# A two-layer Fourier and RG-LRU trunk on one core: position rows loaded by DMA, the first stage in another order, two weight sums on VectorE, zero-frequency columns written at once

## The chip, the cores and the metric

The kernel runs on one core of one Trainium2 chip. The metric is the device time of one execution in microseconds (us). Engines are named as in the profile: PE (TensorE matmuls), PEld (its weight loads), DVE (VectorE), ACT (ScalarE), POOL (GpSimd), and SPq, the queue on which SyncE issues all DMAs.

## What is computed

128 prompt tokens and 1024 sample tokens of width 1024 pass two layers. Only layer 0 and its input matter here. The position embedding is added to the sample tokens alone: its first 512 columns depend on the row of a token in a 64-wide grid, its last 512 on the column.

```python
xs = x_sample + _grid_pos_embed(...)           # rows: sin, cos(r*omega); columns: sin, cos(c*omega)
h  = _rmsnorm(x, norm_g) * (1 + scale) + shift # shift, scale, gate = split(silu(cond) @ w_ada + b_ada)
u, z = split(h @ w_in)
f  = real(fft2(u, axes=(tokens, 256 channels of a group), norm="ortho"))
y  = einsum("bsgi,gij->bsgj", f, w_fmix) + b_fmix
x  = x + gate * ((y * silu(z)) @ w_out)
```

## The kernel before

Every wide product is three matmuls on a value split in a high part (`...h`, rounded by ACT) and the rest (`...l`, by DVE): helper `mm3`, lines 238 to 240, or the same by hand.

The **first stage** transforms the tokens before they meet `w_in`. Token tiles `x0` (prompt) to `x8` get their position rows and their norm; `x1..x4` are paired with `x5..x8` into a difference `d0..d3` and a sum that stays in place. `psO` are the products of the differences with DFT tables (`dh`, `dl` from `dr`), one PSUM tile for each of 8 column blocks; `psT` and `psF` do the same on differences and sums of the sums. ACT and DVE scale them by `coef` and write them as `Qo` and `Qr`, the transformed tokens. Beside this `fold` multiplies the DFT of the channels into `w_fmix` (tiles `wf`, results `Ah Al Bh Bl R`), and `ada_part` computes scale (`s0..s3`) and shift (`h0..h3`) from 16 tiles `wada`: eight matmuls for a pair of tiles, then a copy `hot` (ACT), a small product `adc` (PE) and `coef` (DVE).

The first stage is planned: class `Plan` puts DVE, ACT and POOL operations in order by costs written in the code; where an operation has two costs, it may go to DVE or POOL. PE and the DMA queue keep the order of three strings. `DORD` is the order of loads (`x` token tiles, `w` the `wf`, `t` DFT tables, `s` and `h` the `wada`, `p` position rows, `L` the first pair of `w_u0`). `PORD` and `RORD` are the order on PE: `j` pairs of tiles, `f` folds, `t62` means 6 column blocks with `d2`, `u52` block 5 with `d0, d1`, `o` the eviction into `Qo`, `q` the `psT`, `F` the `psF`, `U` the first two products `pu` of the mixer. Buffers are few: two `dr`, three `raw` (for `wf`, the second half of `wada`, `w_u0`), four `xs` (`x5..x8` and the first half of `wada`), eight PSUM banks. A load waits on SPq for its buffer, and everything behind it waits too.

Position rows come as one 80x512 table. DVE marks six one-hot blocks in `hot`, six matmuls spread the table over 128 tokens, ACT copies four of the results to SBUF, two stay in PSUM. `pos0` and `pos1` add them to a tile; `pos0` is tied to DVE.

The **mixer** runs over 8 channel groups g: `umat(g)` (`pu`) multiplies `Qo` and `Qr` by the sums and differences `e`, `o` of two weight tiles `uL`, `uR` (made by `uweights(g+1)` on POOL), `ymat(g-1)` applies `A`, `B`, `R` and stores `y`. In g=0, `prologue` computes the Nyquist channel (`nyq`, `Ucat`) and a row of norm factors `rb` from nine diagonal blocks `dg`. `norm_stream`, three (chunk, k) pairs per g, makes the normed tokens for z on POOL (`nt`) and stores them in `hD`; after g=7 they are loaded again (`hr`, `hh`, `hl`) for the z stage. Here and after, the Tile framework's scheduler orders each engine. `zero(c)` overwrites the zero-frequency columns of `Qr[c]` from `k0r`, high part and rest, in two small DVE operations for each of 8 column blocks.

Of the kernel before, what the change touches and what calls it, by code (L numbers as in the profile page):

```python
# [187 lines left out]
def body(tc, nc, a):  # L188
# [211 lines left out]


    hot = xp.tile([128, 512], F32, name="hot")
    posR, posC = [None] * 4, [None] * 2
    for n, (kind, i) in enumerate((("R", 0), ("C", 0), ("R", 2), ("C", 1), ("R", 1), ("R", 3))):
        oh = hot[:, i * 128:i * 128 + 128]
        lo, hi = (0, 64) if kind == "C" else (64, 80)

        def mark(kind=kind, i=i, oh=oh, lo=lo, hi=hi):
            if kind == "C":
                e = ident[lo:hi, 32 * i:32 * i + 32].rearrange("p (o c) -> p o c", o=1).broadcast_to([64, 4, 32])  # L410
            else:
                e = ident[lo:hi, 64 + 4 * i:68 + 4 * i].rearrange("p (r o) -> p r o", o=1).broadcast_to([16, 4, 32])
            V.tensor_copy(oh[lo:hi].rearrange("p (r c) -> p r c", r=4), e)

        def spread(n=n, kind=kind, i=i, oh=oh, lo=lo, hi=hi):
            T["ps", f"p{n}"] = ps(f"pos{kind}{i}")
            PE.matmul(T["ps", f"p{n}"], oh[lo:hi], T["dr", "pos"][lo:hi], start=True, stop=True)
# [2 lines left out]
        if kind == "R" and i % 2 == 0:  # L420
            posR[i] = ("ps", f"p{n}")
        else:
            key = (posC if kind == "C" else posR)[i] = ("pos" + kind, i)

# [1149 lines left out]
```

## Time and profile before

| | |
|---|---|
| three runs | 1504.72 us median (1499.46 to 1507.64) |
| the profiled execution | 1498.54 us, of which the span is 1496.8 us |
| PE, DVE, ACT, POOL busy in it | 97%, 72%, 49%, 11% |

The span runs from the first to the last instruction. Shares are means over stages with different limits: a change in one stage is read from the waits in that stage. The granted clock column shows 1.00 also where no record exists, as in the first 20 us.

### The profile page before, as it was taken

What the parts mean: (1) busy time and instruction counts of PE and PEld (TensorE: products, weight loads), DVE (VectorE), ACT (ScalarE), POOL (GpSimd) and SP (SyncE); (2) the same over time, 40 slices, a digit from 0 to 9 for tenths busy, and PEclk for the clock granted to TensorE, in tenths of its full rate; (3) what the DMA queues carried; (4) which work ended last, traced back from release to release, by engine and by line L of the source; (5) the groups of instructions that cost most, each with busy time, mean ns of one, the idle gap of its engine ahead of it and who ended that gap; (6) DMA issues with size and microseconds to landing.
All of it is one profiled execution on the core that took longest, in us unless ns stands there. A gap on an engine that the chain in (4) does not pass through costs nothing. (4 is left out here: it accounts for less than half of the span.)

```text
span 1496.8 us, 21486 instructions
## 1 busy us (share of the span) xinstructions
PE 1452.2 (97%) x8370; PEld 1414.3 (94%) x8370; DVE 1073.2 (72%) x1596; ACT 740.5 (49%) x1113; POOL 157.5 (11%) x165
## 2 busy tenths in 40 slices
PE   7888999999999999999999999999999999999996
PEld 4578999999999999999999999999999999899996
DVE  7775455798864486747888787878788888686453
ACT  6552233322222354526866666666675758464331
POOL 2026785000001001000000000000000000000000
PEclk9998999999999999999999999999999999999998
DMA  6643657887665567531111111111111111786451
GB/s 222 200 130 117 178 188 266 302 269 247 223 212 162 184 195 240 187 126 43 59 59 60 57 59 58 59 59 58 59 59 59 59 58 65 231 287 206 148 189 48
DMA packets 83926, 212.73 MB, mean 142 GB/s; under 512 B 11424, under 2 KB 42656, under 8 KB 83696
## 3 DMA queue, kind: packets, MB, share of 16 engines
q1 hardware_dynamic: 83824, 211.36, 43.2%
q8 instruction: 65, 1.06, 0.3%
q14 instruction: 37, 0.30, 0.1%
HBM read 171.98 MB, written 39.35 MB: 141 GB/s over the span
## 5 line engine op out<-in xcount | busy, mean ns | idle before, releaser
L270 DVE SCALAR_TENSOR_TENSOR sil1j<-wada,sil 128x1024 bf16<-128x1024 f32 x64 | 78.1, 1220 | 9.9 <-DMA wada<-w_ada 9.8
L1289 DVE SCALAR_TENSOR_TENSOR uc<-u,tab,uc 128x1156 f32<-128x1156 f32 (+2 forms) x54 | 69.3, 1288 | 15.7 <-ACT u L1272 14.4
L1348 DVE SCALAR_TENSOR_TENSOR nu<-ga,nu 128x1156 f32<-128x1156 f32 x32 | 43.5, 1358 | 47.4 <-ACT tr L1343 47.3
L1107 DVE SCALAR_TENSOR_TENSOR x<-o,ada,xr 128x128 f32<-128x128 f32 (+1 forms) x64 | 31.6, 513 | 58.1 <-PE o L240 57.5
L1326 ACT ACTIVATE tr<-g,gb 128x386 f32<-128x386 f32 (+1 forms) x96 | 54.8, 584 | 22.0 <-PE g L240 21.0
L227 ACT CAST gh<-gr 128x384 fp32r<-128x384 f32 x80 | 39.7, 511 | 49.6 <-DMA gr<-gD 48.4
L1275 ACT ACTIVATE uc<-u,tab 128x386 f32<-128x386 f32 (+1 forms) x48 | 32.3, 673 | 61.4 <-PE u L240 61.4
L792 POOL TENSOR_TENSOR xr<-xr,tab 128x384 f32<-128x384 f32 (+1 forms) x24 | 23.0, 961 | 367.6 <-DMA xr<-xT 334.3
L228 DVE TENSOR_TENSOR gl<-gr,gh 128x384 fp32r<-128x384 f32 x80 | 42.1, 555 | 24.0 <-ACT gh L227 24.0
L1401 ACT ACTIVATE szz<-zz 128x386 f32<-128x386 f32 (+1 forms) x48 | 23.6, 495 | 71.9 <-PE zz L240 71.8
L1371 POOL COPY st<-nu 128x1 f32<-128x1 f32 x16 | 6.8, 426 | 495.5 <-DVE nu L1370 495.4
L888 ACT CAST uh<-pu 128x256 fp32r<-128x256 f32 (+1 forms) x32 | 12.7, 398 | 84.9 <-PE pu L240 84.8
L1326 ACT ACTIVATE ti<-g,gb 128x386 f32<-128x386 f32 (+1 forms) x96 | 51.6, 579 | 5.8 <-PE g L240 5.7
L889 DVE TENSOR_TENSOR ul<-pu,uh 128x256 fp32r<-128x256 f32 (+1 forms) x32 | 14.4, 454 | 49.7 <-ACT uh L888 49.6
L1358 DVE SCALAR_TENSOR_TENSOR ti<-ti,uc 128x1156 f32<-128x1156 f32 x32 | 43.5, 1358 | 7.6 <-ACT ti L1326 7.3
L1332 ACT ACTIVATE nu<-tr,sp2p 128x1156 f32<-128x1156 f32 x32 | 43.5, 1358 | 1.5 <-ACT tr L1326 0.4
L1354 DVE SCALAR_TENSOR_TENSOR tr<-ga,tr 128x1156 f32<-128x1156 f32 x32 | 43.5, 1361 | 0.7
L1362 DVE TENSOR_TENSOR ti<-ti,tr 128x1156 f32<-128x1156 f32 x32 | 43.4, 1357 | 0.4
L1336 ACT ACTIVATE ga<-tr,sm 128x1156 f32<-128x1156 f32 x32 | 43.2, 1349 | 0.1
L1373 DVE TENSOR_TENSOR_SCAN nu<-ga,tab,ti 128x1155 f32<-128x1155 f32 x16 | 41.9, 2619 | 0.1
L1370 DVE TENSOR_TENSOR_SCAN nu<-ga,ti 128x1156 f32<-128x1156 f32 x16 | 40.9, 2559 | 0.3
L227 ACT CAST gh<-sz 128x384 fp32r<-128x384 f32 x16 | 8.2, 514 | 63.1 <-DVE sz L1009 63.1
(1818 smaller groups left out, 5611.1 us busy)
## 6 DMA issues: line engine op xcount, KB each, us to landing
wo<-w_out SPq DMA_DIRECT2D x96, 512.0 KB, 4.2
wz<-w_z SPq DMA_DIRECT2D x32, 512.0 KB, 4.3
wada<-w_ada SPq DMA_DIRECT2D x32, 512.0 KB, 4.3
gr<-gD SPq DMA_DIRECT2D x80, 192.0 KB, 4.2
yD<-y SPq DMA_DIRECT2D x16, 576.0 KB, 4.8
zy<-yD SPq DMA_DIRECT2D x16, 576.0 KB, 6.9
wada<-w_adaN SPq DMA_DIRECT2D x16, 512.0 KB, 5.4
wu<-w_u SPq DMA_DIRECT2D x16, 512.0 KB, 3.6
```

The source lines that it names most:

```text
L227: A.copy(hi, src)
L228: (eng or V).tensor_tensor(lo, src, hi.bitcast(F32), op=ALU.subtract)
L270: V.scalar_tensor_tensor(junk, w, 0.5, sil[:, q, :], op0=ALU.mult, op1=ALU.mult, accum_out=ada[:, layer, mt, q:q + 1])
L1289: V.scalar_tensor_tensor(T["uc", m][:, lo:hi], T[ut][:, lo + t:hi + t], convw[:, m, t:t + 1], T["uc", m][:, lo:hi], op0=ALU.mult, op1=ALU.add)
L1326: A.activation(T[tg, n][:, lo:hi], T["ps", p][:, 0:hi - lo], AF.Tanh, scale=0.5, bias=gb2[:, 2 * d + mat, m:m + 1])
L1332: A.activation(T["nu", n], T["tr", n], AF.Tanh, scale=sp2[:, d, m:m + 1], bias=sp2[:, d, m:m + 1])
L1336: A.activation(T["ga", n], T["tr", n], AF.Exp, scale=sm4[:, d, m:m + 1], bias=sm4[:, d, m:m + 1])
L1348: V.scalar_tensor_tensor(T["nu", n], T["ga", n], 1.0, T["nu", n], op0=ALU.add, op1=ALU.mult)
L1354: V.scalar_tensor_tensor(T["tr", n], T["ga", n], 1.0, T["tr", n], op0=ALU.add, op1=ALU.mult)
L1358: V.scalar_tensor_tensor(T["ti", n], T["ti", n], 1.0, T["uc", m], op0=ALU.add, op1=ALU.mult)
L1362: V.tensor_tensor(ti, ti, T["tr", n], op=ALU.mult)
L1373: V.tensor_tensor_scan(nu[:, 0:L][:, ::-1], ga[:, 0:L][:, ::-1], ti[:, 0:L][:, ::-1], h0[:, 1, m:m + 1], ALU.mult, ALU.add)
```

## The change

The string table moves loads and blocks; the position rows become six 128x512 tiles in DRAM, loaded by six DMAs (two resident for the columns, two buffers for four row tiles), so the marks, the six matmuls, the four copies and the two PSUM banks go; both adds may run on POOL. In `uweights`, groups 1 and 2 make `e` and `o` on DVE. All `Qr` high parts lie in one tile `Qrt[0]`, all rests in `Qrt[1]`, and `zero` writes all columns in two operations. The `rb` part of `prologue` becomes `rows()`, called behind `ymat(0)` in g=1, and the norm stream runs four pairs per g from g=1 to g=6.

```diff
-DORD = 'p a x1 c x5 x6 x2 w0 t0 t1 x8 w1 x3 w3 x7 w2 s0 t2 t3 s1 x4 s2 ... t4 s6 q s7 x0 h0 t5 h1 ...'
-PORD = 'j0 f0 t40 f1 j1 f2 u42 t41 f3 s0 u52 j2 s1 t62 j3 t63 s2 s3 o0 h0 u74 u64 o3 ...'
-RORD = 'h2 F2 F0 F4 h3 F5 F3 F1 F7 U0 F6 U1'
+DORD = 'p4 a x1 p2 p0 c x5 w0 x2 x6 p5 w1 t0 t1 p1 x3 x7 w2 t2 s0 w3 p3 s1 t3 x4 h0 h1 x8 s2 s3 ... t5 t6 x0 h4 ...'
+PORD = 'j0 f0 t40 f1 j1 f2 s0 t41 f3 s1 u52 u42 j2 t62 s2 j3 t63 s3 h0 u64 o1 o0 u74 h1 ...'
+RORD = 'h2 F7 F0 F2 F5 h3 F3 F1 F4 F6 U0 U1'
...
+    def f_pos(n):
+        kw = dict(tag="pos", bufs=2) if n < 4 else {}
+        xa(fetch((posR + posC)[n], lambda: xp.tile([128, 512], F32, name=f"pos{n}", **kw), a["pos"][n], 256))
...
-        xa(P.add("DVE", 0.22, mark, w=[("hot", n)]))
-        xa(P.add("PE", 1.9, spread, r=[("hot", n), ("dr", "pos")], w=[("ps", f"p{n}")]))
...
-            xa(P.add("DVE", 0.68, pos0, port=pk[0] != "ps", r=[pk], w=[x]))
+            xa(P.add("DVE", (0.68, 1.29), pos0, r=[posR[(t - 1) // 2]], w=[x]))
...
-        Qr.extend([[p.tile([128, 2, NF - 256], F32R, name=f"Qr{i}{c}") for i in "hl"] for c in range(KD)])
+        Qrt.extend(p.tile([128, KD, 2, NF - 256], F32R, name=f"Qr{i}") for i in "hl")
+        Qr.extend([[t[:, c] for t in Qrt] for c in range(KD)])
...
-    for c in range(KD):
-        P.add("DVE", 0.3, lambda c=c: zero(c), r=[("k0r", c)], w=[("Qr", c)])
+    def zero():
+        kh = Qrt[0][:, :, 0, 128:258:129]
+        V.tensor_copy(kh, k0r)
+        V.tensor_tensor(Qrt[1][:, :, 0, 128:258:129], k0r, kh.bitcast(F32), op=ALU.subtract)
+    P.add("DVE", 0.4, zero, r=ke, w=[("Qr", c) for c in range(KD)])
...
-            PL.tensor_tensor(e, L, Rr, op=ALU.add)
-            PL.tensor_tensor(L, L, Rr, op=ALU.subtract)
+            eng = V if g < 3 else PL
+            eng.tensor_tensor(e, L, Rr, op=ALU.add)
+            eng.tensor_tensor(L, L, Rr, op=ALU.subtract)
...
-            for c, k in ns[3 * g:3 * g + 3]:
+            if g == 1:
+                rows()
+            for c, k in ns[4 * max(g - 1, 0):4 * g] if g < G - 1 else ():
```

How the strings move work is seen on the engines at three places. First SPq, the loads ahead of `x4` and `x8`. Before (`x_295` is `x8`, `x_250` is `x2`, `x_534` is `x4`, `wada_367` and `wada_520` are the pair of `s0`):

```order
L348 DMA x_295<-x_all 128x1024
L348 DMA wf_302<-w_fmix 128x1024
L348 DMA x_310<-x_all 128x1024
L348 DMA wf_316<-w_fmix 128x1024
L348 DMA x_336<-x_all 128x1024
L348 DMA wf_351<-w_fmix 128x1024
L348 DMA wada_367<-w_adaN 128x1024
L348 DMA dr_381<-tdft 128x512
L348 DMA dr_395<-tdft 128x512
L348 DMA wada_520<-w_adaN 128x1024
L348 DMA x_534<-x_all 128x1024
L348 DMA wada_558<-w_adaN 128x1024
```

The same stretch now (`x_402` is `x4`, `x_442` is `x8`, `wada_326` and `wada_371` are the pair of `s0`, `wada_418` and `wada_428` that of `h0`, `pos_355` a tile of position rows):

```order
L348 DMA dr_315<-tdft 128x512
L348 DMA wada_326<-w_adaN 128x1024
L348 DMA wf_343<-w_fmix 128x1024
L348 DMA pos_355<-pos 128x512
L348 DMA wada_371<-w_adaN 128x1024
L348 DMA dr_391<-tdft 128x512
L348 DMA x_402<-x_all 128x1024
L348 DMA wada_418<-w_adaN 128x1024
L348 DMA wada_428<-w_adaN 128x1024
L348 DMA x_442<-x_all 128x1024
L348 DMA wada_480<-w_adaN 128x1024
```

`x8` has moved from far ahead of the first `wada` to behind `x4`, and two tiles of the `xs` buffers are free for the pair of `s0` before `x8` takes one.

Second ACT, around the copy `hot` that follows `s3`. Before (`x_644` is `x0`):

```order
L433 CAST d_3h<-d_594 128x1024
L450 CAST dh_639<-dr_613 128x512
L480 ACTIVATE jk_668,nc_209<-x_644 128x1024
L483 ACTIVATE nc_209<-nc_209,eps 128x1
L484 ACTIVATE nc_209<-nc_209,epsh 128x1
L578 COPY hot<-ada_560 128x512
```

And now (`x_701` is `x0`):

```order
L411 CAST d_3h<-d_589 128x1024
L428 CAST dh_621<-dr_594 128x512
L555 COPY hot<-ada_466 128x512
L593 ACTIVATE Qoh_170<-psO_347,coef 128x512
```

The square of `x0` has moved behind `hot` and six evictions.

Third DVE and PE where the mixer first reads `Qr`. On PE before, with the waits of a row in brackets, at the first product of the differences `o` with `Qr` (`pu_1_1`) and the first of the sums `e` (`pu_0_1`):

```order
L238 MATMUL pu_1_1_1096<-Qrh_824,o0h 128x322
L239 MATMUL pu_1_1_1096<-Qrl_825,o0h 128x322
L240 MATMUL pu_1_1_1096<-Qrh_824,o0l 128x322
L238 MATMUL pu_0_1_1095<-Qrh_814,e0h 128x322 [waits DVE_49,PE_49]
L239 MATMUL pu_0_1_1095<-Qrl_815,e0h 128x322 [waits DVE_49]
```

And now, at the same place:

```order
L240 MATMUL pu_1_0_996<-Qoh_184,o0l 128x256
L238 MATMUL pu_1_1_1052<-Qrh,o0h 128x322 [waits DVE_49,PE_49]
L238 MATMUL pu_0_1_1051<-Qrh,e0h 128x322
L239 MATMUL pu_1_1_1052<-Qrl,o0h 128x322 [waits DVE_49]
L240 MATMUL pu_1_1_1052<-Qrh,o0l 128x322
```

On DVE now, the rows up to the two writes of the zero columns (8x2 columns each; `uL_1036` are weights of group 1, whose sums `e` and `o`, lines 835 and 836, stand a few rows above):

```order
L228 TENSOR_TENSOR e1l<-e_1040,e1h 128x1024
L868 TENSOR_TENSOR ul_1_1108<-pu_1_0_996,uh_1_1107 128x256
L742 TENSOR_TENSOR k0r<-k0r,kb 128x16
L597 SCALAR_TENSOR_TENSOR Qrl<-psF_939,coef,Qrh 128x2x65
L597 SCALAR_TENSOR_TENSOR Qrl<-psF_930,coef,Qrh 128x2x65
L228 TENSOR_TENSOR o1l<-uL_1036,o1h 128x1024
L786 MEMSET zt 128x1024
L747 CAST Qrh<-k0r 128x8x2
L748 TENSOR_TENSOR Qrl<-k0r,Qrh 128x8x2
```

Before, a product with `o` waited for no zero column; now the first one waits for DVE at a point behind the write of the high columns (the row after it, which reads those columns, waits for nothing more), and on DVE that write stands behind all the work on the weights of group 1.

## Rows read from the trace of the kernel before

**Rows 1.** Stretches: length, busy PE, PEld, DVE, ACT, POOL, clock, DMA share, GB/s.
```profile
20.30:70.30 50.00, 44.12 (x194) 30.74 (x196) 40.62 (x58) 29.60 (x55) 9.71 (x5) 0.97 0.59 206
107.00:130.00 23.00, 16.26 (x83) 14.96 (x82) 16.91 (x37) 4.81 (x8) 8.43 (x4) 0.70 0.22 69
148.00:232.00 84.00, 84.00 (x632) 84.00 (x631) 43.28 (x116) 25.05 (x50) 63.26 (x60) 1.00 0.64 195
262.00:1400.00 1138.00, 1132.14 (x6440) 1127.03 (x6439) 868.57 (x1167) 607.16 (x864) 34.99 (x56) 1.00 0.41 134
```

**Rows 2.** Waits of PE from 20 to 262 us: total, times, longest.
```profile
PE pu L239 <- DVE Qrl L770: 4.0, 2, 3.7
...
PE qb L238 <- ACT p L906: 2.9, 1, 2.9
...
PE adc L583 <- ACT hot L578: 2.4, 1, 2.4
...
PE psO L238 <- DVE Bl L540: 2.1, 1, 2.1
...
PE pu L238 <- DVE Qrh L769: 1.9, 1, 1.9
...
PE pu L240 <- DVE e0l L437: 1.1, 1, 1.1
...
PE pu L239 <- DVE Qrl L620: 0.8, 1, 0.8
```

**Rows 3.** Waits of the DMA queue, 20 to 62 us.
```profile
SPq L348 <- DVE x L505: 23.1, 3, 18.9
```

**Rows 4.** Timeline of PE: start, length, operation, count, wait before it.
```profile
46.60 2.15 PE L568 MATMUL ada<-wada,silZ 128*32 128x512 f32 x8
...
53.27 2.94 PE L568 MATMUL ada<-wada,silZ 128*32 128x512 f32 x8
...
77.55 1.06 PE L568 MATMUL ada<-wada,silZ 128*32 128x512 f32 x8
...
98.83 0.38 PE L238 MATMUL pu<-Qoh,e0h 128*128 128x256 f32 x1 [0.81 <-ACT e0h L433]
```

**Rows 5.** Timeline of ACT around the copy hot.
```profile
67.09 1.06 ACT L480 ACTIVATE jk<-x 128x1024 bf16<-128x1024 f32 x1 [6.15 <-DMA x<-x_all]
...
68.66 0.56 ACT L578 COPY hot<-ada 128x512 f32<-128x512 f32 x1
```

**Rows 6.** Stretches that hold a time at the lower clock.
```profile
51.00:55.00 4.00, 4.00 (x10) 1.52 (x10) 2.90 (x7) 1.63 (x4) 0.00 (x0) 0.57 0.68 224
92.50:96.00 3.50, 3.50 (x18) 3.50 (x18) 0.88 (x4) 0.48 (x1) 2.36 (x1) 0.52 0.02 6
112.90:126.60 13.70, 8.91 (x34) 7.96 (x34) 9.70 (x25) 0.62 (x2) 4.72 (x2) 0.50 0.29 92
```

**Rows 7.** Timelines of POOL and DVE: one POOL operation and its DVE neighbour.
```profile
24.08 1.40 POOL L471 TENSOR_TENSOR x<-x,posC 128x512 f32<-128x512 f32 x1 [23.64 <-DMA x<-x_all]
...
24.25 2.31 DVE L502 SCALAR_TENSOR_TENSOR d<-x,rs,x 128x1024 f32<-128x1024 f32 x1
```

**Rows 8.** Timeline of DVE ahead of the zero columns.
```profile
100.29 1.27 DVE L620 SCALAR_TENSOR_TENSOR Qrl<-psF,coef,Qrh 128x258 fp32r<-128x258 f32 x4
...
104.39 0.67 DVE L828 TENSOR_SCALAR dg<-tab,rs 128x128 f32<-128x128 f32 x3
...
105.54 5.52 DVE L828 TENSOR_SCALAR dg<-tab,rs 128x128 f32<-128x128 f32 x6
...
114.05 0.91 DVE L809 MEMSET zt<- 128x1024 f32 x1 [0.15 <-DVE Qrh L769]
...
114.95 1.22 DVE L228 TENSOR_TENSOR o1l<-uL,o1h 128x1024 fp32r<-128x1024 f32 x1
```

**Rows 9.** Timeline of POOL in the same time, and its waits from 130 to 262 us.
```profile
105.74 2.52 POOL L856 TENSOR_TENSOR e<-uL,uR 128x1024 f32<-128x1024 f32 x1 [2.94 <-DMA uR<-w_u]
...
POOL nt L792 <- DMA nt<-xT: 22.4, 14, 5.7
```

More of the change, by code (lines that the diff above doesn't have):

```diff
@@ L334, in ps @@
         return pp.tile([128, 512], F32, tag="ps", name=name)
-    P = Plan({"raw": 3, "hi": 4, "lo": 4, "xs": 4, "d": 2, "dr": 2, "dh": 4, "ps": 8}, fixed=("SP", "PE"), handles={"DVE": V, "POOL": PL})
+    P = Plan({"raw": 3, "hi": 4, "lo": 4, "xs": 4, "d": 2, "dr": 2, "pos": 2, "dh": 4, "ps": 8}, fixed=("SP", "PE"), handles={"DVE": V, "POOL": PL})
     T, xa_ops = {}, []
@@ L375, in f_ada @@
             xa(fetch(("xs", f"wada{part}{k}"), lambda: xp.tile([128, D], F32, tag="xs", name=f"wada{part}{k}", bufs=4), src, 512))
+    posR, posC = [("pos", i) for i in range(4)], [("posC", 4 + i) for i in range(2)]
+    def f_pos(n):
+        kw = dict(tag="pos", bufs=2) if n < 4 else {}
+        xa(fetch((posR + posC)[n], lambda: xp.tile([128, 512], F32, name=f"pos{n}", **kw), a["pos"][n], 256))
     pdc = xb.tile([128, 130], F32, name="pdc")
@@ L399, in body @@
     P.add("ACT", 0.4, silu, w=[("silT", 0)])
[L402 to L417, printed above, removed]
-        xa(P.add("DVE", 0.22, mark, w=[("hot", n)]))
-        xa(P.add("PE", 1.9, spread, r=[("hot", n), ("dr", "pos")], w=[("ps", f"p{n}")]))
[L420 to L423, printed above, removed]
-            def keep(n=n, key=key):
-                T[key] = xp.tile([128, 512], F32, name=key[0] + str(key[1]))
-                A.copy(T[key], T["ps", f"p{n}"])
-            xa(P.add("ACT", 0.58, keep, r=[("ps", f"p{n}")], w=[key]))
     def split_ops(src, n, name, pick=lambda t: t):
@@ L569, in mms @@
                               start=j == 0, stop=j == 3, tile_position=(0, g))
-        i = P.add("PE", 1.5, mms, r=names + [("silZ", 0)], w=[p])
+        i = P.add("PE", 1.1, mms, r=names + [("silZ", 0)], w=[p])
         if not part:
@@ L576, in rows @@
             def rows():
-                T[row] = hot if not part else xb.tile([128, D], F32, tag="d", name="arow", bufs=2)[:, 0:512]
+                T[row] = xb.tile([128, 512], F32, name="hot") if not part else xb.tile([128, D], F32, tag="d", name="arow", bufs=2)[:, 0:512]
                 A.copy(T[row], T[p])
@@ L596, in cols @@
                         V.scalar_tensor_tensor(o, o, 1.0, rowed(normg[:, 0, ms]), op0=ALU.add, op1=ALU.mult)
-            k = [P.add("ACT", 0.58, rows, r=[p] + [("hot", n) for n in range(6)], w=[row]),
+            k = [P.add("ACT", 0.58, rows, r=[p], w=[row]),
                  P.add("PE", 1.0, turn, r=[row, ("silZ", 0)], w=[pt])]
@@ L717, in body @@
     norm(0)
-    Qr = []
+    Qr, Qrt = [], []
     hqb_cm = pool("hqb")
@@ L821, in prologue, with rows @@
                 V.tensor_tensor(Ucat[32:64, lo:hi], pu[i][32:64, 0:hi - lo], Ucat[32:64, lo:hi].bitcast(F32), op=ALU.subtract)
+        def rows():
             for c, (lo, hi) in enumerate(OC):
@@ L1501, in constants @@
     posc = np.concatenate([np.sin(ac), np.cos(ac)], 1)
-    out = dict(tdft=tdft, pdft=pdft, fdft=fdft, alt=alt, pos=np.concatenate([posc, posr], 0),
+    out = dict(tdft=tdft, pdft=pdft, fdft=fdft, alt=alt, pos=np.stack([np.repeat(posr[4 * i:4 * i + 4], 32, 0) for i in range(4)] + [np.tile(posc[32 * i:32 * i + 32], (4, 1)) for i in range(2)], 0),
                posRT=posr.T.reshape(4, 128, 16).transpose(1, 0, 2), posCT=posc.T.reshape(4, 128, 64).transpose(1, 0, 2),
```

15 lines of the change are left out of this document (5 added, 10 removed).

## The prediction

> **What bounds the kernel now.** I read the busy shares of the page first: PE is busy for 97% of the span and no other engine for more than 72% (the table in the section on time). A change can therefore only win where PE stands still or runs slowly. The stretches say where that is [rows 1]. From 262 to 1400 us PE works 1132 of 1138 us, and from 148 to 232 us all the time, so neither part can win much, and a second gained ahead of them arrives at the end as long as nothing else holds them. All that the change touches lies before 262 us. There PE works 44.1 of 50.0 us from 20.3 to 70.3 us and 16.3 of 23.0 us from 107 to 130 us. Then the waits of PE, with the name of what came last [rows 2], and last the clock: three stretches show a granted clock near half [rows 6], that is the 1.2 GHz level in place of 2.4 GHz, each behind a wait.
>
> **First stage, to 70.3 us.** The position matmuls lie ahead of the first fold, where PE has nothing else to do, so taking them away gains nothing by itself: the first fold waits for `wf0h` and `wf0l`, behind the norms of `x1` and `x5` on ACT and DVE. ACT loses two short copies ahead of `wf0h`, DVE the marks; but `x1` now waits for one more load. I set this at zero, with 1 us either way.
>
> The gain is behind it. SPq stood 18.9 us on one DVE operation, the sum `x2 + x6` that frees an `xs` buffer [rows 3], and the second `wada` of `s0`, `x4` and the next `wada` were issued only after it. So `s0` took 2.15 us where an undisturbed one takes 1.06 [rows 4]: 1.1 us. In the new order both tiles of `s0` find a free buffer or one freed by `x5`, and `x4` stands behind two DFT tables and no `xs` buffer. Next, block 5 of the tokens waited 2.1 us for a PSUM bank, until DVE had evicted a fold [rows 2]. Two banks that held position rows are now free, and only two blocks are asked for, after all folds: I count the 2.1 us as gone. Then the clock was low, so that `s1` took 2.94 us, 1.9 too many [rows 4], and the 2.3 us before it ran at a granted clock of 0.57 [rows 6], 1.0 too many. Both follow from the two waits. Last, `adc` waited 2.4 us for `hot` [rows 2]: ACT stood 6.15 us on the load of `x0` for a square that was queued ahead of it, and `hot` came behind [rows 5]. Now `hot` is ahead of that square; what is left is the copy itself, 0.56 us, and its handover, together 0.7. That is 1.7 us. Sum: 1.1 + 2.1 + 1.9 + 1.0 + 1.7 = 7.8 us.
>
> Against it stands POOL. Four position adds and the rest of `wf3` go there, three of the adds (about 1.4 us each, [rows 7]) as soon as `x3` and `x7` land, and those now come right behind `w1` and the DFT tables, about when DVE makes `d_0l` and `wf0l`. A difference on DVE that started 0.2 us after such an add took 2.31 us [rows 7], while an operation of that width alone takes about 1.2 [rows 8]: it waited for the add's end. I take one add ahead of `wf0l`, 1.3 us, which leaves **6.5 us** for this stage (with none 7.8, with all three 3.6; and 9 if the start gains its 1 us).
>
> The Trainium skill (SBUF — State Buffer, section "SBUF: two separate sides") says that VectorE and GpSimd share a port pair as an exclusive lock, and that the loser is blocked for the whole instruction when VectorE reads two SBUF inputs. The row agrees with that. By this rule alone all three adds would come between DVE's operations, and this stage would gain 3.6 us in place of 6.5; DVE's small norm operations and the arrival of `x7` one load after `x3` make one the likelier here.
>
> **Second part, 70.3 to 107 us.** The same products in another order. The first product of the mixer waited 0.81 us for `e0h` [rows 4]; `e0` is now made by DVE (1.2 us, [rows 8]) and not by POOL (2.5 us, [rows 9]), and one more `psF` stands ahead of the product: 0.8 us gone. The 3.5 us at a clock of 0.52 [rows 6] cost 1.7 us and followed the waits around `h3`, which mostly stay; I take half of it: **1.7 us** together. The wait for `e0l`, 1.1 us [rows 2], stays. Bounds 0 and 4.
>
> **The zero columns, 107 to 130 us.** Before: waits of 4.0 + 1.9 + 0.8 = 6.7 us for parts of `Qr` [rows 2], and 8.9 us of PE work at half clock [rows 6], which costs 4.5 us: 11.2 us lost. Sixteen small operations become two, but the first product with `Qr` now waits for the last column, where six blocks of `o` went ahead before. PE finishes its products with `Qo` about 7 us after the first of them (98.83 us to 107, [rows 4], without the `psF` that stood between). DVE is done with `e0l` about 1.6 us after that first product, then has, before the zero columns: eight `psF` evictions (four in 1.27 us) 2.5; nine `dg` (three in 0.67) 2.0; `e`, `o` of group 1 and their rests, four times 1.22, 4.9; the memset 0.9 [rows 8]; two evictions of `pu` and some dozen operations of a few columns, estimated at 1.5. That is 11.8 us. POOL still makes `o0l`, and six `dg` took 5.52 us while POOL worked on the weights [rows 8, 9], where they would take 1.3: I add 1.3 us. So the zero columns are ready 1.6 + 11.8 + 1.3 = 14.7 us after that product, and PE stands 14.7 - 7 = 7.7 us in one piece. Behind it the clock is low for some 5 us of work, 2.5 us lost (more than the 1.7 of a short stretch, less than the 4.5 with further stops, [rows 6]). Gain 11.2 - 7.7 - 2.5 = **1.0 us**. Bounds: a wait of 4 us, if DVE runs part of this list before `e0l` and meets no lock (gain 4.7); 12 us, if the weights of group 1 land that much late (loss 3.3). The `rb` products move behind `ymat(0)` and cost PE the same there.
>
> **The mixer, to 262 us.** Its last products waited 2.9 us for an eviction on ACT [rows 2], which stood behind a cast of normed tokens that had come late from POOL's stream. The stream now stops one group earlier, so this wait goes: **2.9 us**, with the bound in the first rival below.
>
> **Sum.** 6.5 + 1.7 + 1.0 + 2.9 = 12.1 us. The profiled execution took 1498.54 us, which gives 1486.4. The median of the runs is 6.2 us above it; a median of the changed kernel can lie as far above its best, and I give 1489.
>
> **Rivals.**
> POOL becomes late. `norm_stream` now begins only after g=1's products, at about the same time as before in spite of the gain ahead of it, and has a sixth less groups to end in. POOL was busy 63 of 84 us [rows 1] and stood 22.4 us for `nt` loads [rows 9]. Against it: four of its weight operations (10 us by [rows 9]) now lie ahead of the stream, and four on DVE. If it keeps all its waits it ends some 6 us earlier than before while PE is 9.2 us earlier: 3.2 us of new wait on top of the 2.9 us that stay. 12.1 - 2.9 - 3.2 = 6.0 us, 1495 by the same median. Chance 0.08.
>
> The first stage gains little: the new SPq order has its own stops (a DFT table behind a rest that POOL makes, `x8` behind two `wada` of the shift, which need the rests of `wf1` and `wf2`), or the adds on POOL come in threes as above. `d3` then comes late and block products wait as they did: 2 us in place of 6.5, so 7.6 us in all or less, 1494 to 1497. For it speaks that DVE is busy 40.6 of 50 us [rows 1], against it that `x4` had to be awaited before. Chance 0.12.
>
> The one-tile wait decides: on DVE, in order, the zero columns stand behind the sums of group 1, and those behind the load of `uR`. A wait of 7.7 + 12.1 = about 20 us would eat the whole gain, one of 28 us makes the kernel slower by over 0.5%, about 1508. It needs that load some 20 us later than DVE is ready; before, POOL waited 2.94 us for it [rows 9]. Chance 0.06, other losses included.
>
> **Chances and range.** 0.5% (7.5 us) is about what a measurement of this kernel can tell from no change. My forecast has 0.74, all of it faster by over 0.5%; the first two rivals, 0.20, are the same; the last, 0.06, is slower. The terms at their best ends give 9 + 4 + 4.7 + 2.9 = 20.6 us, 1478 from the profiled execution; the two middle rivals reach 1497 and a little over with the spread of the runs. The range is 1479 to 1500.
>
> **What would show it.** Right: `s0` and `s1` near 1.06 us, no wait of `psO` on `Bl`, `adc` behind `hot` by less than 1 us and ended near 64 us; one wait of PE on DVE of about 8 us at the first `Qr` product, a stretch at the lower clock after it, the second group's products starting near 119 us; no long wait of `qb`. Wrong: a wait of the third fold matmul on `wf0l` of several us, waits on `d_2l` or `d_3l`, SPq standing on POOL for the fourth DFT table, a longer `Qr` wait, or PE waiting on `hl` or `p` near 250 us.

## The result, and the profile after

17 runs of each on the same chips: 1511.5 us median (1508.31 to 1515.28) against 1502.99 us (1497.16 to 1507.64) before, a ratio of 1.0053 with a 95% interval of 1.0042 to 1.0064. The change is slower by about half a per cent. Its profiled execution took 1508.31 us, with a span of 1506.5 us against 1496.8.

PE was ahead up to the end of the mixer and lost its lead there. First the waits of PE from 20 to 262 us after the change, as in [rows 2] (total, times, longest):

```profile
PE qb L238 <- ACT p L885: 12.1, 2, 11.4
PE pu L238 <- DVE Qrh L747: 7.1, 1, 7.1
PE pa L238 <- ACT p L885: 5.6, 1, 5.6
...
PE pu L240 <- DVE e0l L415: 0.8, 1, 0.8
...
PE adc L560 <- ACT hot L555: 0.7, 1, 0.7
```

`psO` no longer waits for a bank, `adc` waits 0.7 us in place of 2.4, and the four waits for parts of `Qr` are one of 7.1 us. But the wait for `p` (the ACT eviction of the products `pa`) at the end of the mixer, 2.9 us before, has become 17.7 us in three pieces. When each of these places is reached is seen in the timeline of PE (start, length, operation, wait before it; compare [rows 4]):

```profile
38.81 1.07 PE L545 MATMUL ada<-wada,silZ 128*32 128x512 f32 x8
...
46.52 1.06 PE L545 MATMUL ada<-wada,silZ 128*32 128x512 f32 x8
...
62.44 1.05 PE L560 MATMUL adc<-sel,hot 128*128 128x4 f32 x8 [0.69 <-ACT hot L555]
...
89.33 0.39 PE L238 MATMUL pu<-Qoh,e0h 128*128 128x256 f32 x1 [0.28 <-ACT e0h L411]
...
103.52 0.61 PE L238 MATMUL pu<-Qrh,o0h 128*128 128x322 f32 x1 [7.10 <-DVE Qrh L747]
...
117.18 0.28 PE L238 MATMUL pu<-Qoh,e1h 128*128 128x256 f32 x1
...
241.38 0.58 PE L238 MATMUL pa<-uh,Ah 128*128 128x256 f32 x1 [5.59 <-ACT p L885]
...
257.92 0.64 PE L238 MATMUL qb<-uh,Bh 128*128 128x322 f32 x1 [11.44 <-ACT p L885]
...
258.89 0.53 PE L238 MATMUL z<-hh,wz0h 128*128 128x384 f32 x1
```

`s0` and `s1` take 1.07 and 1.06 us. The lead of PE is 6.8 us at `adc`, 9.5 us at the first product of the mixer and 14.4 us at group 1 (`pu<-Qoh,e1h`, before at 131.58 us), of which 1.6 us are the `rb` products that come later now. Then 14.8 us of added waits and two stretches at the lower clock (the rows of 1.2 GHz below: start:end and length, busy PE, PEld, DVE, ACT, POOL, then clock, DMA share, GB/s) turn it into a lag: the first `z` product starts at 258.9 us, 3.7 us later than before, where it read:

```profile
255.16 0.34 PE L238 MATMUL z<-hh,wz0h 128*128 128x384 f32 x1
```

The two slow stretches of the change:

```profile
241.00:245.00 4.00, 3.62 (x15) 3.62 (x16) 2.78 (x11) 1.53 (x4) 3.38 (x4) 0.52 0.93 350
257.90:262.00 4.10, 4.08 (x13) 4.08 (x14) 2.10 (x6) 2.91 (x7) 0.00 (x0) 0.51 1.00 403
```

What is late is found by going back from the wait. On ACT, in order, the eviction `p` stands behind a cast of reloaded normed tokens:

```profile
256.57 0.92 ACT L227 CAST hh<-hr 128x384 fp32r<-128x384 f32 x2 [14.04 <-DMA hr<-hD]
257.40 0.89 ACT L885 ACTIVATE p<-pa,tab 128x256 f32<-128x256 f32 x2
```

On SPq that load of `hr` stands behind the last two stores of the norm stream, and the stream began late (timeline of SPq, first the change, then before):

```profile
134.23 0.33 SPq L832 DMA_DIRECT2D uR<-w_u  x1
134.65 0.38 SPq L820 DMA_DIRECT2D nt<-xT  x1
...
249.94 2.04 SPq L826 DMA_DIRECT2D hD<-nt  x2
253.57 2.22 SPq L935 DMA_DIRECT2D hr<-hD  x3
```

```profile
130.78 1.62 SPq L842 DMA_DIRECT2D nt<-xT  x3
...
247.75 0.32 SPq L848 DMA_DIRECT2D hD<-nt  x1
250.01 2.27 SPq L954 DMA_DIRECT2D hr<-hD  x3
```

Behind the last store the load waits another 1.6 us for POOL's first `hl`, which frees its buffer and which POOL makes only when the whole stream is done (waits of SPq from 245 to 258 us):

```profile
SPq L935 <- POOL hl L228: 2.4, 2, 1.6
```

The first `nt` load left at 130.8 us before; now it leaves at 134.65 us, although PE is 14 us ahead. The `nt` tiles share three buffers with the `dg` tiles that the `rb` products read, and these products come behind `ymat(0)` now. PE's rows of the `rb` products, first before, then the change:

```profile
129.94 2.10 PE L829 MATMUL rb<-dg,ones 128*128 128x384 f32 x6
```

```profile
133.75 2.10 PE L807 MATMUL rb<-dg,ones 128*128 128x384 f32 x6
```

Both times the load leaves 0.8 to 0.9 us after the first of them starts; the scheduler also put the load behind the weights of two more groups. POOL, freed of the first sums, stood waiting for a load in the time that it had won:

```profile
118.16 2.40 POOL L835 TENSOR_TENSOR e<-uL,uR 128x1024 f32<-128x1024 f32 x1 [25.10 <-DMA uR<-w_u]
...
141.55 0.61 POOL L769 TENSOR_TENSOR nt<-nt,tab 128x256 f32<-128x256 f32 x1 [8.44 <-DMA nt<-xT]
...
251.61 3.84 POOL L228 TENSOR_TENSOR hl<-hr,hh 128x384 fp32r<-128x384 f32 x4
```

From 258.9 us to the end another 6 us are lost. About 1.5 us are the rest of the slow stretch (3.1 us of work at 0.51). Another 2.5 us are short waits of the output products `o` for reloaded tiles and weights (`gh` 2.1 us in four pieces against 0.5 in two, `wo1040h` 2.3 against 1.4). From 1300 us to the end the granted clock is 0.96 in place of 0.98; which wait lowered it is not shown.

### The profile page after: what moved, and what is told of

It is laid out like the page before. It is cut to its first block, busy times and chain, and to the rows that moved or that the text cites. A ratio compares the mean times of both kernels' runs of the same rounds, so it can differ in the third digit from the quotient of the medians.

```text
span 1506.5 us, 21430 instructions
## 1 busy us (share of the span) xinstructions
PE 1438.0 (95%) x8358; PEld 1411.9 (94%) x8358; DVE 1066.9 (71%) x1579; ACT 739.1 (49%) x1109; POOL 148.8 (10%) x162
## 3 DMA queue, kind: packets, MB, share of 16 engines
q8 instruction: 65, 1.06, 0.3%
## 5 line engine op out<-in xcount | busy, mean ns | idle before, releaser
L270 DVE SCALAR_TENSOR_TENSOR sil1j<-wada,sil 128x1024 bf16<-128x1024 f32 x64 | 78.0, 1219 | 10.3 <-DMA wada<-w_ada 10.3
L1270 DVE SCALAR_TENSOR_TENSOR uc<-u,tab,uc 128x1156 f32<-128x1156 f32 (+2 forms) x54 | 69.3, 1288 | 15.7 <-ACT u L1253 14.4
L988 ACT ACTIVATE sz<-z 128x384 f32<-128x384 f32 x48 | 23.1, 487 | 50.7 <-PE z L240 30.0
L868 DVE TENSOR_TENSOR ul<-pu,uh 128x256 fp32r<-128x256 f32 (+1 forms) x32 | 14.4, 453 | 40.7 <-ACT uh L867 40.7
```

The lines of the kernel that those rows point to most:

```text
L270: V.scalar_tensor_tensor(junk, w, 0.5, sil[:, q, :], op0=ALU.mult, op1=ALU.mult, accum_out=ada[:, layer, mt, q:q + 1])
L1270: V.scalar_tensor_tensor(T["uc", m][:, lo:hi], T[ut][:, lo + t:hi + t], convw[:, m, t:t + 1], T["uc", m][:, lo:hi], op0=ALU.mult, op1=ALU.add)
```

## The experiments

**Theory S**: the norm stream, from its first `nt` load to its last store, takes some 110 to 120 us whatever PE does, and its end sets when the end of the mixer and the `z` products can run; so the change lost by starting it later. **Rival W**: POOL was made late by the sums on VectorE. Others came up on the way. All kernels and what decides them, by the profiles (us) and the ratio to before with its 95% interval; "gap" is from the issue of the last store to the first `z` product:

| kernel | first pu | first nt load | last store | first z | gap | span | ratio |
|---|---|---|---|---|---|---|---|
| before | 98.8 | 130.8 | 247.8 | 255.2 | 7.4 | 1496.8 | 1 |
| before again (b2) | 94.3 | 128.2 | 249.1 | 256.5 | 7.4 | 1500.7 | 1.0002 (0.9984 to 1.0021) |
| the change | 89.3 | 134.6 | 251.7 | 258.9 | 7.2 | 1506.5 | 1.0053 (1.0042 to 1.0064) |
| e1 old stream | 91.3 | 120.6 | 241.6 | 249.0 | 7.4 | 1496.2 | 0.9956 (0.9941 to 0.9970) |
| e2 before, late stream | 96.2 | 145.0 | 261.4 | 268.5 | 7.1 | 1512.2 | 1.0077 (1.0060 to 1.0095) |
| e4 rows early | 92.8 | 121.0 | 241.6 | 249.1 | 7.5 | 1500.7 | 0.9955 (0.9939 to 0.9972) |
| e5 sums on POOL | 91.1 | 136.4 | 254.8 | 262.0 | 7.2 | 1513.1 | 1.0061 (1.0044 to 1.0077) |
| e3 first stage only | 91.9 | 122.4 | 250.2 | 257.6 | 7.4 | 1506.0 | 1.0005 (0.9992 to 1.0019) |
| e8 e1, sums on POOL | 91.8 | 122.7 | 242.4 | 249.9 | 7.5 | 1496.1 | 0.9955 (0.9940 to 0.9970) |
| e9 e1, columns one by one | 92.1 | 114.6 | 240.1 | 249.3 | 9.2 | 1499.5 | 0.9947 (0.9931 to 0.9964) |
| e10 e1, rb product on DVE | 91.7 | 120.4 | 251.6 | 274.1 | 22.5 | 1519.0 | 1.0086 (1.0063 to 1.0109) |
| e11 e1, stores by POOL | 90.7 | 119.7 | 252.3 | 241.4 | none | 1500.5 | 0.9988 (0.9969 to 1.0007) |
| e12 e1, hl on DVE | 90.6 | 119.2 | 242.3 | 251.0 | 8.7 | 1497.5 | 0.9977 (0.9962 to 0.9992) |
| e13 e1, loads too by POOL | 91.2 | 122.5 | 280.4 | 240.0 | none | 1510.1 | 1.0049 (1.0032 to 1.0067) |
| e15 e1, no additions | 90.3 | 118.7 | 233.1 | 244.3 | 11.2 | 1489.3 | 0.9945 (0.9925 to 0.9964) |
| e16 e3, no additions | 89.0 | 120.4 | 233.3 | 243.9 | 10.6 | 1491.6 | 0.9929 (0.9908 to 0.9950) |
| e18 before, no additions | 98.6 | 130.6 | 242.9 | 253.2 | 10.3 | 1497.5 | 0.9956 (0.9940 to 0.9972) |
| e17 e1, scale late | 90.9 | 120.2 | 233.8 | 259.5 | 25.7 | 1515.7 | 1.0037 (1.0021 to 1.0052) |
| e19 e17 and e9 | 91.8 | 115.2 | 233.5 | 258.9 | 25.4 | 1506.7 | 1.0044 (1.0028 to 1.0060) |
| e20 e1, all sums on DVE | 92.9 | 121.1 | 224.0 | 257.4 | 33.4 | 1505.2 | 0.9971 (0.9954 to 0.9988) |

The columns before the ratio are of one profiled execution each, which can lie several us from the median of its runs: e17 7.1 and e20 6.5 us over it, e15 5.5 us under it. The ratio is of all runs. From the first load to the last store the stream takes 116 to 128 us in the nine kernels from before to e8.

### Where the stream starts

**e1, the change with the old stream.**

```diff
             if g == 0:
                 prologue()
+                rows()
-            if g == 1:
-                rows()
-            for c, k in ns[4 * max(g - 1, 0):4 * g] if g < G - 1 else ():
+            for c, k in ns[3 * g:3 * g + 3]:
```

> The change with its norm stream as before: the row rb made in the prologue, three pairs per group from g=0. Theory S (the stream starts too late, because rb now stands behind the products of group 1, and the end of the mixer waits for the stream's end): the first nt load leaves SPq near 119 us in place of 134.65, the stream ends near 234 us in place of 251.6, the two waits of PE for p (5.6 and 11.4 us) shrink to 3 us or less together, and the span falls by 14 to 20 us to 1487 to 1492, some 7 us under before. Rival W (POOL is late because the sums on DVE leave it waiting 25.1 us for the load of uR): the stream ends no more than 5 us earlier and the span stays above 1500.

**e2, before with the new stream**: the same edit the other way round, in the kernel before.

> The kernel before with nothing changed but the norm stream: rb behind the products of group 0's y in g=1, four pairs per group from g=1. Theory S: rb is made near 146 us, the stream ends near 262 us in place of 247.7, PE waits for p about 15 us longer at the end of the mixer, and the span rises by 14 to 18 us to 1511 to 1515. Rival W: the sums stay on POOL, so the stream ends within 4 us of before and the span stays within 4 us of 1496.8.

**e4, the change with only `rows()` back in the prologue**:

```diff
             if g == 0:
                 prologue()
+                rows()
-            if g == 1:
-                rows()
```

> The change with rb made in the prologue, but the stream left at four pairs per group from g=1. It tells the place of rb from the place of the stream's calls. Theory S in its narrow form (the place of rb decides, since the nt tiles share their buffers with the tiles that make rb and the scheduler orders the rest): the first nt load near 119 us, no long wait for p, span 1487 to 1492 as with all of the old stream. Its wide form (the calls from g=1 on and the four per group decide): a span within 4 us of 1506.5. Rival W: above 1500.

**e5, the change with the sums back on POOL.**

```diff
-            eng = V if g < 3 else PL
+            eng = PL
```

> The change with the sums of groups 1 and 2 back on POOL, all else as changed. Two things at once, in different places. At the zero columns, theory Z (the two writes stand on DVE behind the sums and rests of group 1): the wait of PE at the first Qr product falls from 7.1 us to 2 to 3 us. At the end of the mixer, theory S: the stream starts no later than the earlier PE makes it, so what is gained at the zero columns is given back in the wait for p; span within 4 us of 1506.5. Rival W: POOL gets its weights in time, the waits for p shrink by 10 us or more, span 1490 to 1495.

e1 and e4 start the stream 14 us earlier, at 121 us, and come out alike, 0.45% under before. So the place of `rb` matters and the four calls per group do not: in both, the load leaves 0.8 us after the first `rb` product. The waits of PE for `p` in e1 (130 to 262 us):

```profile
PE pa L238 <- ACT p L885: 3.2, 1, 3.2
PE qb L238 <- ACT p L885: 2.4, 1, 2.4
```

e2 has none of the change's other parts and loses more than the whole change does, 0.77% against 0.53% (waits of PE, 200 to 285 us):

```profile
PE qb L238 <- ACT p L908: 11.7, 1, 11.7
PE pa L238 <- ACT p L908: 5.3, 1, 5.3
```

So late rows of `rb` cost 14.6 us (0.97%, e1 against the change; 0.77% in e2), and theory S holds for their place. W falls: with the sums on POOL (e5) the stream ends 3 us later, not earlier. Two things were off. The stream in e1 ended at 241.6 us and not at 234, and its span was 1496.2 us and not 1487 to 1492: it is not only the start that counts, and 5.6 us of waits for `p` stayed. And in e5 the wait at the zero columns fell only to 5.0 us, not 2 to 3, and a new one of 2.7 us (`nyq` for `w8h`) came behind it. The rows of VectorE and of POOL say why.

```profile
98.33 1.53 DVE L739 TENSOR_TENSOR k0r<-k0r,coef 128x16 f32<-128x16 f32 x1
...
100.05 2.23 DVE L742 TENSOR_TENSOR k0r<-k0r,kb 128x16 f32<-128x16 f32 x1
```

```profile
97.47 2.35 POOL L835 TENSOR_TENSOR e<-uL,uR 128x1024 f32<-128x1024 f32 x1 [2.67 <-DMA uR<-w_u]
99.91 2.35 POOL L836 TENSOR_TENSOR uL<-uL,uR 128x1024 f32<-128x1024 f32 x1
```

Each of these small operations ends when POOL's does; in the change `L739` takes 0.17 us and `L742` 0.16 us.

### What the parts bring under the stream

With the old stream, parts were taken away: **e3** has none of the sums on VectorE and no joint columns, **e8** lacks the sums, **e9** the joint columns (the edit of e5, and the `Qr` tiles and `zero(c)` of before).

```diff
-        Qrt.extend(p.tile([128, KD, 2, NF - 256], F32R, name=f"Qr{i}") for i in "hl")
-        Qr.extend([[t[:, c] for t in Qrt] for c in range(KD)])
+        Qr.extend([[p.tile([128, 2, NF - 256], F32R, name=f"Qr{i}{c}") for i in "hl"] for c in range(KD)])
...
-    P.add("DVE", 0.4, zero, r=ke, w=[("Qr", c) for c in range(KD)])
+    for c in range(KD):
+        P.add("DVE", 0.3, lambda c=c: zero(c), r=[("k0r", c)], w=[("Qr", c)])
```

> Of the change only the new strings, the position rows by DMA and the planner's costs; the weight sums back on POOL, the zero columns column by column, rb and the norm stream as before. The lead of PE at the first pu product is that of the change (about 91 us against 98.8), and the stream starts as much earlier as PE. If the end of the mixer is set by the stream (theory S), the lead that VectorE sums and two-operation columns give before it is worth nothing there, so this kernel comes within 2.5 us of the change with the old stream (ratio to before 0.994 to 0.9975). If PE's own path sets it, this kernel is 4 to 6 us slower than that (ratio 0.998 to 1.0).

> The change with the old norm stream and all weight sums on POOL; the columns stay in two operations. POOL has four more operations of 2.4 us ahead of the stream. Theory S: the stream ends 2 to 5 us later than with the sums on VectorE (241.6 us there), PE waits that much longer for p, ratio to before 0.997 to 0.999. If POOL has slack there, no difference: 0.9945 to 0.9965. At the first Qr product PE waits 5 us, as VectorE's small operations before the columns take 1.5 to 2.3 us in place of 0.17 while POOL makes the sums.

> The change with the old norm stream and the zero columns column by column, in tiles of their own; the sums stay on VectorE. At the columns PE has six blocks of o to go on with, so one wait of 7.1 us becomes several of 1 to 4 us, 3 to 8 us in all, with a stretch at the lower clock. If the stream sets the end of the mixer (theory S), the total stays within 2.5 us of the change with the old stream (ratio 0.994 to 0.9975), whatever PE gains or loses at the columns; if PE's own path does, the total follows the columns.

e8 and e9 equal e1 within the intervals, as S has it: what PE gains ahead is covered. e3 does not fit: its stream starts with that of e8 (122.4 and 122.7 us) and ends 8 us later, so PE waits 11.0 us for `p`, not 5.0, and the whole gain is gone. The two streams run together to their twelfth store (192.1 us and 192.4); the next load leaves at 195.7 us in e3 and 193.1 in e8, and the nineteenth store at 235.0 and 227.4. Between these the two queues SPq differ in a few places (a store of `y` between two loads of `wz`, a reload of `hr` ahead of a store). That these cost the 8 us was not tried.

### What sets the stream's pace

All in e1. **e10**: the product with `rb` on VectorE (first pair of lines). **e11**: the stores issued by POOL (second pair), **e13** the loads as well (second and third). **e12**: the rests `hl` of the first tiles on VectorE (fourth). **e15**: no additions of the position rows (last line), so part of the computation is left out.

```diff
-            PL.tensor_tensor(t, t, rb[:, lo:hi], op=ALU.mult)
+            V.tensor_tensor(t, t, rb[:, lo:hi], op=ALU.mult)
...
-            SY.dma_start(hD[c][k // 2][:, k % 2, :], t)
+            PL.dma_start(hD[c][k // 2][:, k % 2, :], t)
...
-            SY.dma_start(t, a["xT"][k][:, lo:hi])
+            PL.dma_start(t, a["xT"][k][:, lo:hi])
...
-                split(r[:, j, :], h, lw, PL if c == 0 and k + j < 4 else V)
+                split(r[:, j, :], h, lw, V)
...
-            add_pos(t, k, lo, hi)
```

> The change with the old norm stream, in which the product with rb (24 operations of 1.02 us on POOL) is made by VectorE. What sets the stream's pace? If POOL's work does, the stream ends 8 to 20 us earlier than 241.6 us, the waits for p (5.6 us there) go below 1.5 us and the ratio to before falls to 0.988 to 0.992. If the loads and stores of the three nt tiles in their order on SPq do (a rival), the stream ends within 4 us of 241.6 and the ratio stays at 0.994 to 0.998.

> The change with the old norm stream, whose 24 stores to hD are issued by POOL itself, right behind the operation that ends a tile, and not by SPq, where they stand behind other queued transfers. In all ten profiles so far the z products start 7.1 to 9.2 us after the stream's last store. Theory Q (the order of SPq holds the stream): POOL's wait for nt loads falls from 22.3 us to under 12, the last store leaves 8 to 15 us earlier than 241.6 us, the waits for p (5.6 us) go, ratio to before 0.990 to 0.993. Rival: issuing from POOL costs POOL time (over 0.5 us each) and the stream ends within 3 us of 241.6 or later, ratio 0.995 or more.

> The change with the old norm stream and the rests hl of the first four normed tiles on VectorE in place of POOL, where they stand behind the whole stream and keep the raw buffers of the next hr loads. If these four operations are a part of the 7.4 us between the last store and the first z product, that gap shrinks by 1.5 to 2.5 us and the z products start 1.5 to 2.5 us earlier; ratio to before 0.993 to 0.996. If the stores on SPq alone hold the hr loads, the gap stays at 7 us or more.

> As the one with the stores on POOL's queue, and the 24 loads of nt are issued by POOL too. A load then waits for the store of the tile before it in its buffer, and POOL stands while it does. Theory Q in its full form (SPq's order is all that holds the stream): as early an end as with the stores alone or earlier, ratio 0.990 to 0.993. If a load needs its buffer's store to land (some 2 us each) with POOL standing, the stream ends later than with stores alone by 5 us or more, ratio above 0.995.

> The change with the old norm stream, which leaves out the addition of position rows to the normed tokens of z (24 operations of 0.6 to 1.0 us on POOL, some 20 us in all; part of the computation is left out). If POOL's own work sets the stream's pace as much as the transfers do, the last store leaves 6 to 15 us earlier than 241.6 us, the waits for p go and the z products start as early as PE can reach them, about 243 us; the span falls by 5 to 7 us to 1489 to 1491, ratio about 0.992. That is then what the first stage, the sums and the zero columns are worth when the stream doesn't hide them. If the transfers alone set the pace: last store within 4 us of 241.6 us, ratio 0.995.

e15 says that POOL's work is part of the pace: 22 us less of it up to 262 us, and the last store leaves 8.5 us earlier; the waits for `p` fall to 3.0 us and the profiled span to 1489.3, though the ratio, 0.9945, is no lower than e1's within its interval. Theory Q of the queue's order falls: in e11 POOL's waits for loads fell only from 22.3 to 19.8 us, its 24 issues took 0.59 us each, and the stream ended 11 us later. Yet PE did not wait for `p` at all in e11 and e13, where no store of the stream stands ahead of the `hr` loads on SPq: so it is these stores that tie the end of the mixer to the end of the stream. Nothing was won by it, since PE then stood for `hl`, which POOL makes behind the stream (8.4 us in e11, 5.4 in e13), and for `hh` (1.9 and 11.9 us). In e13 POOL also stood 17.1 us for its own stores to land. The Trainium skill (DMA: Bandwidth & Descriptors, "Issuing engines are not separate DMA queues") says that the transfers run on the same 16 DMA engines whichever engine issues them; these runs agree in so far as another issuer gave no speed. e12 shortened nothing: with `hl` on VectorE the `hr` load leaves 0.4 us after the last store in place of 1.9, but lands 4.3 us later in place of 3.2. e10 was a surprise, slower by 0.86%: POOL hands each tile to VectorE, and VectorE, in order, waits with all that PE needs behind it (waits of DVE, then of PE, 100 to 262 us):

```profile
DVE nt L822 <- POOL nt L769: 52.5, 10, 18.1
```

```profile
PE qb L238 <- DVE ul L868: 24.1, 4, 13.0
```

One stop of the stream was not tried. Behind g=2 the program stores two vectors `silD` of 4 KB each. In the change the DMA engines are busy almost all of the time from 181 to 195 us, though they move only 1.73 MB, in 2982 packets of which 2189 are under 512 B. The two stores of the stream issued beside them land after 11.2 and 11.3 us (median of its 24 stores 2.6), and POOL then waits longest (10.4 us; 5.7 in before, 11.6 in e1):

```profile
181.33 0.32 SPq L826 DMA_DIRECT2D hD<-nt  x1
181.70 1.29 SPq L925 DMA_DIRECT2D silD<-silT  x2
```

```profile
194.72 0.83 POOL L769 TENSOR_TENSOR nt<-nt,tab 128x384 f32<-128x384 f32 x1 [10.41 <-DMA nt<-xT]
```

All twenty profiles have this place: a transfer issued beside `silD` took 9.8 to 17.7 us to land. How much earlier the stream would end without it is open.

### Unhidden

The last six: **e18** and **e16** are before and e3 without the stream's additions (the last line of the diff above), and leave out the same part; **e17** moves the stream's scale and shift behind the reload, on VectorE (first part below), **e19** does so in e9; **e20** has the sums of all groups on VectorE (second part); **b2** is the kernel before, profiled again.

```diff
-            for s, e, q in segments(lo, hi):
-                PL.tensor_scalar(t[:, s - lo:e - lo], ..., sc_a(0, k, q), sc_b(0, k, q), ...)
             SY.dma_start(hD[c][k // 2][:, k % 2, :], t)
...
+                for s, e, q in segments(*OC[c]):
+                    V.tensor_scalar(r[:, j, s - lo:e - lo], ..., sc_a(0, k + j, q), sc_b(0, k + j, q), ...)
                 split(r[:, j, :], h, lw, PL if c == 0 and k + j < 4 else V)
```

```diff
-            eng = V if g < 3 else PL
+            eng = V
```

> Of the change only the first stage (strings, position rows by DMA, costs), with the stream as before but without the addition of position rows in it (24 operations on POOL; part of the computation is left out). With the stream's additions this kernel came out the same as before (ratio 1.0005), its stream ending at 250.2 us and PE waiting 11 us for p. If the stream hides the first stage's gain, the last store leaves 8 to 16 us earlier, the waits for p fall under 4 us, and the span falls from 1506.0 to 1492 to 1498, ratio 0.992 to 0.996. If the first stage is worth nothing at the end for another reason, the ratio stays above 0.998.

> The kernel before without the addition of position rows in its stream (part of the computation is left out). If before was held by its stream only by the 2.9 us that PE waits for p, it gains 2 to 4 us (ratio 0.997 to 0.999) and no more. If the stream's end held more than that wait shows, 5 us or more (ratio under 0.997). The first stage without those additions minus this one is what the first stage is worth unhidden: 4 to 8 us by PE's lead of about 7 us at the first product of the mixer.

> The change with the old norm stream; the scale and shift of a normed tile (32 operations of 0.45 to 1.0 us, some 21 us of POOL) move out of the stream to VectorE, behind the reload of the tile, ahead of its split. Nothing is left out. If POOL's work per tile sets the stream's pace, the last store leaves 6 to 12 us earlier than 241.6 us, the waits for p go under 3 us, the z products start near 243 to 246 us, ratio 0.991 to 0.994. If VectorE's added work (some 12 us between 225 and 275 us) comes ahead of what PE waits for, the z products wait for hh or hl in its place and the ratio stays at 0.995 or above.

> As the one before, and the zero columns column by column in tiles of their own, as in the kernel before the change. Unhidden by the stream, the two forms of the zero columns can be compared: by the waits of PE there (7.1 us in one piece against 4.6 us in pieces) the pieces are 1 to 3 us faster; if the total follows, this is the fastest version, ratio 0.990 to 0.993. If the stream still sets the end, no difference.

> The change with the old norm stream, and the weight sums of all groups on VectorE, not only those of groups 1 and 2. POOL loses ten more operations of 2.4 us in the mixer and VectorE gains ten of 1.2 us that wait for loads issued well ahead. If POOL's work sets the stream's pace, its last store leaves 5 to 12 us earlier than 241.6 us, the waits for p (5.6 us) fall under 3 us and the ratio to before is 0.990 to 0.994. If VectorE, which also makes the rests ul that PE waits for, is held by a late uR load or by POOL's operations beside it, PE waits for ul in its place (as when the stream's product or scale was put there) and the ratio is 0.997 or more.

> The kernel before once more, for a second profile of it. The forecast took its first profile, 1498.54 us, as the frame, 6.2 us under the median. If that execution was a typical one, the second has the same waits: 2.9 us of PE for p, z products from 255 us, span 1495 to 1499. If the stream ends later in a typical execution, PE waits 5 to 10 us for p, the z products start at 258 to 262 us and the span is 1500 to 1505.

Without the additions the first stage comes through: the first `z` product 9.3 us earlier (e16 against e18), the span 5.9 us shorter, the ratio 0.9929 against 0.9956, about 4 us, with intervals that overlap. With the additions, e3 had shown nothing. The joint columns and the sums added nothing to that (e15 against e16), though PE ran its way from the first `pu` to group 1 in 29.2 us in place of 32.2. Before was held too: e18 gains 0.44%, 6.6 us, more than its profiles show (2.0 us at `z`). And in b2 PE came to the mixer 4.5 us earlier than in the first profile, the stream ended 1.3 us later, and `z` started 1.3 us later; PE waited for `p` (150 to 262 us):

```profile
PE qb L238 <- ACT p L906: 3.5, 1, 3.5
PE pa L238 <- ACT p L906: 2.1, 1, 2.1
```

e17, e19 and e20 show that work can be taken from POOL and the stream ends 7 to 18 us earlier, and yet nothing is won over e1, since each puts on VectorE an operation that waits for a transfer. In e20 it is a sum, whose load of `uR` stands on SPq behind an `nt` load that waits for a store beside `silD` (issued at 160.04 us, landed 11.4 us later; waits of DVE, then PE, in an execution 6.5 us over the median):

```profile
DVE e L835 <- DMA hD<-nt: 14.5, 1, 14.5
```

```profile
PE qb L238 <- DVE ul L868: 12.2, 1, 12.2
```

In e17 it is the scale of a reloaded tile, and PE waited 13.8 us for `ul`. The fastest versions that compute all are e9, e8, e4 and e1, 0.44 to 0.53% under the kernel before and equal within their intervals: the change with `rows()` left in the prologue, with or without the joint columns or the sums.

## Why the prediction was wrong

The forecast was 1489 us in a range of 1479 to 1500; the median is 1511.5. **The step that failed is the fourth term**, "The mixer, to 262 us": "The stream now stops one group earlier, so this wait goes: 2.9 us". It took the order of the calls in the program for an order in time. Moved behind `ymat(0)`, the `rb` products gave up the buffers of the first `nt` loads 3.8 us later than before, although PE was 14 us ahead. And the four tiles per group did not come: the `nt` tiles have three buffers, and the twelfth store left at 206.0 us, against 197.4 before. The wait grew to 17.7 us. The first rival had the mechanism (POOL becomes late) and even the reason, but was sized on the guess that the stream keeps its start of before and its end moves 6 us earlier: 6 us and a chance of 0.08, where start and end both came 3.9 us later. Its "sixth less groups" are six calls in place of eight. The signs that the forecast named for being wrong at this place came: a long wait of `qb`, and PE waiting on `p` near 250 us.

Behind that lies a reading error. The 2.9 us of [rows 2] looked like a small leftover at the end of the mixer. It was the sign that two chains, PE's and the stream's, met there, and that PE's was the shorter: the gap of 7.1 to 7.5 us from the last store to the first `z` product is the same in before, b2, the change and six more kernels (9.2 and 8.7 in e9 and e12), though PE reaches group 1 up to 14 us apart in them. So what was won ahead of it was worth nothing there until the stream moved as well, and the sum of the first three terms could not be carried to the end.

**Term by term.** The sum of the first three terms, as a lead of PE, stood; its parts did not, and that they add up is luck. The first two profiles show 6.8 us at `adc`, where 6.5 were forecast, but `adc` starts at 66.9 to 69.3 us in four profiles of kernels with the old first stage and at 62.1 to 66.3 in 16 with the new one, so one pair of profiles says little. The means of those four and of the ten profiles with all three parts of the change ahead of group 1 are better: 67.9 and 64.3 us at `adc`, 97.0 and 91.2 at the first `pu` product, 130.3 and 120.7 at group 1 (with `rb` counted ahead of it in all). So the first stage gave 3.6 us in place of 6.5, the second part 2.2 in place of 1.7, the zero columns 3.8 in place of 1.0, together 9.6 in place of 9.2. The waits were as told: `s0`, `s1` at 1.07 and 1.06 us, no wait for a bank, `adc` 0.7 us behind `hot` (ended at 63.5 us). Zero columns: one wait of 7.7 us forecast, 7.1 measured, and the order on VectorE was the predicted one (sums, rests, memset, then the columns):

```profile
101.06 1.21 DVE L228 TENSOR_TENSOR o1l<-uL,o1h 128x1024 fp32r<-128x1024 f32 x1
102.43 0.91 DVE L786 MEMSET zt<- 128x1024 f32 x1 [0.16 <-DVE o1l L228]
103.26 0.12 DVE L747 CAST Qrh<-k0r 128x16 fp32r<-128x16 f32 x1
```

The slow stretch behind that wait lasted 5 us of work as forecast:

```profile
103.00:108.40 5.40, 4.88 (x18) 4.91 (x19) 0.57 (x3) 0.00 (x0) 0.00 (x0) 0.51 0.34 99
```

Group 1 started at 117.2 us (forecast near 119).

**The rivals.** "First stage gains little" came in part by the means, 3.6 us where it said 2, but did not decide the time; "the one-tile wait decides" did not come. **The frame**: the first profile of before, 1498.54 us, lay 4.5 us under the median of 17 runs; b2's execution took 1502.46 us, with 5.6 us of waits for `p` in place of 2.9. By these two profiles part of the spread between executions lies in the stream, which the forecast did not see.

**Left open**: why e3's stream ends 8 us after e8's; what the `silD` stores cost; and why the output products wait 1.1 to 4.8 us for `gh` in all kernels with the new first stage, against 0.5 to 1.1 us in the four with the old one. From the first `z` product to the end those four take 1241.6 to 1244.3 us, the new ones (e11 and e13 aside, where `z` begins before the stream ends) 1244.9 to 1256.2 us, so some of what is gained ahead of `z` is given back there.

## What to carry to other kernels

A short wait where a side stream meets the bound engine is not a leftover to be counted once: ask which of the two chains is late there, and price every gain ahead of it at zero there until the stream's start or pace has moved by as much. When a preparation is moved (here `rb`), follow what needs it through every queue to the last reader. And work taken off a slow helper engine should not go ahead of an eviction on an engine that runs in order if it waits for a transfer (e17, e19, e20) or for that helper (e10).

## What the runs showed of the hardware

Two operations of VectorE on 128x16 elements took 1.53 and 2.23 us beside POOL's sums (e5) and 0.17 and 0.16 us without them (the change): beside the sums, both ended with POOL's operation. The Trainium skill (SBUF — State Buffer, "SBUF: two separate sides") says that an operation of VectorE with two SBUF inputs waits for the whole of a GpSimd operation that reads SBUF. The trace agrees. Together they held the zero columns 3.4 us longer, which by this estimate is most of the 5.0 us that PE still waited there when the sums went back to POOL.

POOL issued a DMA in 0.54 to 0.72 us (e11), SPq nine of ten in 0.32 to 0.43 us. Beside two stores of 4 KB, in a stretch with 2189 packets under 512 B, stores of 192 KB took 11.2 and 11.3 us to land, where the median was 2.6 (the change). TensorE kept its higher clock (1.00) behind a wait of 2.9 us in before, and was granted 0.51 to 0.52 behind the waits of 5.6, 7.1 and 11.4 us in the change. Kernels with the same first stage reach `adc` up to 4.2 us apart.
